# First loads in a fixed order with z's first units cut in halves, and the last output tile added and stored in halves, in a hybrid decoder block on one core

## The chip, the core and the metric

The kernel runs on one core of a Trainium2 chip. The core has five engines with instruction streams of their own: TensorE (PE in the profile; its weight loads are PEld), VectorE (DVE), ScalarE (ACT), GpSimd (POOL) and SyncE (SP), which here only issues transfers. Transfers are issued by SP, by ACT or by POOL and run on 16 DMA engines. The metric is the device time of one execution in microseconds (us); less is better. The profile is one profiled execution, and its span is the time from its first to its last instruction.

## The reference

One layer of a decoder block, 512 tokens, model width 1024, float32 throughout:

```
u = RMSNorm(x)
[q_A,k_A,v_A,z_A,a_A,b_A | q_B,k_B,v_B,f_B | gate_A,gate_B] = u @ W_in
A: causal conv(4)+SiLU on q/k/v, L2-norm of q and k, gated delta rule in chunks, per-head RMSNorm * SiLU(z)
B: RMSNorm of q and k per head, causal softmax attention with a bias cumsum(log sigmoid(f))
m = sigmoid(gate_A) * (y_A @ P_A) + sigmoid(gate_B) * (y_B @ P_B);  h = x + m @ W_out
out = h + relu(RMSNorm(h) @ W_up)^2 @ W_down
```

## The kernel before

Every product is made in three matmuls of rounded parts: each operand is split into a high part (a cast on ACT, type fp32r) and a low part (a subtraction on DVE), and PE adds high times high, low times high and high times low. The weights come in units of 128 x 1024 numbers (512 KB). `seq` lists the units in the order of their use: first `w_ab` (128 x 256, the gates' columns), then five units of `w_z`, then those of `w_gdn` and so on. A unit is loaded into a `raw` tile (`load`, line 209; three buffers of the pool `wraw`), split into `hi` and `lo` (`prefetch_split`, line 258) and used by `unit` and `dense`.

The front of the kernel runs like this. VectorE sets `ones`, ACT copies one column of it (`warm`, for its table load), and PE runs ten warm-up matmuls (line 320). The gain `mix_g` is loaded by POOL. x comes transposed in eight tiles `xt[k]` of 128 x 512 (256 KB each). The loop at line 334 issues them on SP, and between them `prefetch_raw(2 + k)` loads the first units: behind x's tile 0 come `w_ab` and both halves of the first `w_z` unit (`cuts`, line 238), behind tile 1 both halves of the second, then tiles 2 to 7, then the third `w_z` unit and the small inputs. The loop at line 405 makes, per tile, the product with the gain as a high part on ACT and a low part on DVE (`split`, lines 304 and 305), splits the units that are due (lines 265 to 272), squares the tile on ACT (line 410) and adds the square to `sqs` on DVE (line 412). Behind it stands the first product stage (lines 415 to 422): per tile of x two matmuls for `w_ab` and three for each of the two `w_z` units, 64 in all, into three PSUM banks. Then `sumsq` (line 366) multiplies `sqs` with `ones`, and `gates` turns the sum into the inverse norm `rs`, spreads it by matmuls with `ident` (line 378) and copies it to `rb` (line 379). The z products are multiplied by `rb` on DVE (line 1070), which frees their banks for the following z units, and `normalise` (line 425) multiplies x by `rb` on POOL and splits it again as `uhi` and `ulo` for all later products. `blk_id` (line 355) is made of four small copies on ACT; a matmul at line 495 is its first reader.

The end of the kernel is the list `MLP`, whose last two steps are the product P4 of the last quarter of `w_d`. `tokens_product` (line 1339) makes, for two blocks of 128 tokens (t = 0, 1), six matmuls of 512 columns each per step. `add_product` yields tasks that scale the PSUM banks and add them to the accumulators `accs` (`add_task`, line 1356, on DVE); `count` calls `give` (line 1454) once both are added, which stores both tiles of 256 KB from SP.

The order of instructions on each engine is not that of the code: a planner orders them by times that it estimates itself. Three things bind it: data dependencies, buffers, and `keep_in_program_order`, which ties an instruction behind the one traced before it on its engine.

Of the kernel before, what the change touches and what calls it, by code (L numbers as in the profile page):

```python
# [15 lines left out]
P = 128  # L16
# [28 lines left out]
def hybrid_block(tc, a, out):  # L45
# [39 lines left out]
    def const(shape, s, dt=F32):  # L85
        return (cp if s in KEEP else cm).tile(shape, dt, tag=s, name=s)
# [52 lines left out]
    def start(gen):  # L139
        tasks.append(gen)  # L140
        return gen
# [67 lines left out]
    def load(n):  # L209
        nme, i = seq[n]  # L210
        if nme in FACTOR:
            w, c, s_ = i
            q, old = FACTOR[nme]
            if old is None:
                if w == "w_st" and c >= NST:
                    raw = fresh[{"P1": 1, "P2": 2, "P3": 0}[nme]].tile([P, D], F32, tag="raw", name=nm("sraw"))
                elif w in ("w_st", "w_sf"):
                    raw = (swp if nme == "P1" else wraw).tile([P, D], F32, tag="raw", name=nm("sraw"))
                else:
                    raw = fresh[2 if nme == "P2" else s_].tile([P, D], F32, tag="raw", name=nm("draw"))  # L220
# [17 lines left out]
        cuts = [slice(0, 512), slice(512, D)] if 0 < n < 3 else [slice(0, w)]  # L238
        for c in cuts:
            nc.sync.dma_start(raw[:, c], a[nme][i][:, c])  # L240
        raws[n] = raw, cuts
# [68 lines left out]
    ones = const([P, P], "ones")  # L310
    vec.memset(ones, 1.0)
    warm = const([P, 1], "warm")
    act.copy(warm, ones[:, 0:1])
    expo = const([P, 16], "expo")
    vec.memset(expo, -0.5)
# [3 lines left out]
    for _ in range(NWARM):  # L319
        mm(pw[:, 0:P], ones, ones, start=True, stop=True)  # L320

    def small_in(name, shape, eng=None):
        t = const(shape, "c_" + name)
        (eng or nc.sync).dma_start(t, a[name])
        return t

    def small_row(name, n):
# [1 line left out]
        nc.sync.dma_start(t, a[name].partition_broadcast(P))  # L329
        return t  # L330

    mix_g = small_in("norm_mix_g", [P, KT], nc.gpsimd)
    xt = [page(s="x") for _ in range(KT)]
    for k in range(KT):
        nc.sync.dma_start(xt[k], a["xT"][k])
# [16 lines left out]
    pool.tensor_scalar(mid[:P // 2, :], upper[:P // 2, :], 1.0, None, op0=ALU.subtract)  # L352
    blk_id = const([P, 32], "blk_id")
    for b in range(4):
        act.copy(blk_id[b * 32:(b + 1) * 32, :], ident[b * 32:(b + 1) * 32, b * 32:(b + 1) * 32])
    fqs = const([P, 1], "fqs")
    pool.tensor_scalar(fqs, fq_g, float(P) ** -0.5, None, op0=ALU.mult)

# [42 lines left out]
    for pool_, tag, n in early:  # L401
        t = pool_.tile([P, n * T], F32R, tag=tag, name=nm("xs"))
        spots += [t[:, i * T:(i + 1) * T] for i in range(n)]
    sqs = page(s="proj")
    for k in range(KT):
        xs.append(split(xt[k], mix_g[:, k:k + 1], dst=spots[2 * k:2 * k + 2] if k < 3 else None))
        if k < 2:
            prefetch_split(2 + k)
        sq = page(s="sq") if k else sqs
        act.activation(sq, xt[k], AF.Square)  # L410
        if k:
            vec.tensor_tensor(sqs, sqs, sq, op=ALU.add)
    first = [unit("w_ab"), unit("w_z"), unit("w_z")]
    fps = [mmps() for _ in first]
    for k in range(KT):
# [642 lines left out]
    gt = start(gates(fps[0]))  # L1058
    tick()
    tick()  # L1060
    def zgate(h):
        if h < len(fps) - 1:
            ps = fps[1 + h]
        elif h < NZX:
            ps = dense("w_z", xh, xl)
        else:
            ps = dense("w_z", uh, ul)
        z = page(s="proj")
        if h < NZX:
            vec.tensor_tensor(z, ps, rb, op=ALU.mult)  # L1070
            ps = z
        act.activation(z, ps, AF.Silu)
        nc.sync.dma_start(zd[h], z)
        tick()
# [8 lines left out]
    for h in range(NZ1, H):  # L1083
# [3 lines left out]
    ahead = []  # L1087
    stream(EARLY, [fox_chunk((None, v01), (0, v01[0])), fox_chunk((2, v23[0]), (1, v01[1])), fox_chunk((3, v23[1]), (None, v23))],
           uforms, lambda c: start(decays(1, box)) if c == "d" else ahead.append(project(G, len(ahead))), False)
    hold[0] = True  # L1090
    ch1 = gdn_group(1, box, ahead=ahead)
    hold[0] = False
# [246 lines left out]
    def tokens_product(c, p, s_, form, ps, first):  # L1339
# [114 lines left out]
    def give(i, l):  # L1454
        for tb in (2 * i, 2 * i + 1):
            nc.sync.dma_start(out[tb][:, l * T:(l + 1) * T], accs[tb][l])

    MADE = {"P2": (("P1", "a"), ("P1", "b")), "P6": (("P2", "a"), ("P2", "b")), "P4": SUMS}
    evicted = []
    for k, (w, c, p, s_) in enumerate(MLP):  # L1460
# [27 lines left out]
        if w == "w_u":  # L1488
            if p == "P1" and s_ == 0:
                mlp[c] = quarters("act"), {}  # L1490
            qs, forms = mlp[c]
            blocks_product(c, p, s_, [hforms[k] for k in needs], ps, first)
            evicted = [(evict, p, qs[s_], ps[s_])]
            if s_ == NSUB - 1 and p in MADE:
                steps = MADE[p]
                if p == "P4" and c == NC - 1:
                    steps = sorted(steps, key=lambda st: ("P5", "P6", "P3", "P7", "P4").index(st[0]))
                evicted.append((forms_later, qs, forms, steps))
        else:
            tokens_product(c, p, s_, res[p, s_], ps, first)  # L1500
            done = h_done if w == "w_o" else give if c == NC - 1 else lambda i, l: None
            evicted = list(add_product(w, c, p, ps, done)) if s_ == NSUB - 1 else []
        evicted += gone
    for f, *args in evicted:
        f(*args)
# [81 lines left out]
```

## Time and profile before

| | |
|---|---|
| median of 3 runs | 966.58 us (966.54 to 966.62) |
| profiled execution | 968.33 us |
| its span | 966.5 us |
| mean granted TensorE clock | 0.998 |
| PE busy | 956.0 us (99%) |
| DVE, ACT, POOL busy | 756.2, 645.0, 219.7 us |
| transfers over the span | 180.38 MB |

Busy times are sums over an engine's instructions where they do not overlap. A row of the order of time names the start and the length in us, the engine, the line, the operation, the tile it writes and those it reads; in brackets stands how long the engine had been idle and what ended it. A row of the stage table has the stretch, its length, busy time and number of instructions for PE, PEld, DVE, ACT and POOL, the granted clock, the busy share of the DMA engines and GB/s. A row of the waits has the waiting instruction, what it waited for, us in total, times, and the longest. In the tables of transfers the last number is us from issue to landing.

### The profile page before, as it was taken

To read this page: it belongs to the slowest core of one execution; us is meant where nothing else is said; L and a number is where in the kernel's file an instruction comes from. 1 tells how busy PE (TensorE), PEld (TensorE's weight loads), DVE (VectorE), ACT (ScalarE), POOL (GpSimd) and SP (SyncE) were. 2 spreads that over 40 slices of the span, in tenths; PEclk is the share of its full clock that TensorE was granted. 3 is DMA by queue.
4 is the path that set the end of the run, shared out by engine and by line. 5 is a ranking of instruction groups with operands and counts; after the bars stand their busy time and mean duration, and the time that the engine had idled before them with its cause. 6 is when DMAs were issued, how large, how long until landed. Compare 5 with 4: busy or idle time off the path is not lost.

```text
span 966.5 us, 17529 instructions
## 1 busy us (share of the span) xinstructions
PE 956.0 (99%) x6634; PEld 873.6 (90%) x6634; DVE 756.2 (78%) x1281; ACT 645.0 (67%) x1096; POOL 219.7 (23%) x224
## 2 busy tenths in 40 slices
PE   8999999999999999999999999999999999999998
PEld 6788889988888999999999899889989989988986
DVE  6877979967488899956656887979886796697696
ACT  7879855678675577888655554678755855666761
POOL 1503222340343243322230110202122021121110
PEclk9999999999999999999999999999999999999999
DMA  8457678854677877858789687878798798788883
GB/s 284 138 160 240 189 177 203 175 167 138 202 244 190 181 162 164 190 119 189 202 185 328 143 221 208 152 186 169 172 216 179 194 166 204 183 174 197 192 170 111
DMA packets 87291, 180.38 MB, mean 187 GB/s; under 512 B 8152, under 2 KB 41048, under 8 KB 87208
## 3 DMA queue, kind: packets, MB, share of 16 engines
q0 software_dynamic: 17392, 63.12, 38.0%
q1 hardware_dynamic: 69816, 116.15, 37.1%
q8 instruction: 52, 0.85, 0.3%
q14 instruction: 31, 0.25, 0.1%
HBM read 160.11 MB, written 19.14 MB: 185 GB/s over the span
## 4 chain that ended last, share of the span: by engine, by line
PE 71%; DVE 3%; issue 2%; ACT 2%; DMA 1%; POOL 0%; POOLq 0%; DVEq 0%
PE mlp L1228 36%; PE st L1003 14%; PE mm L290 4%; PE mm L291 4%; PE mm L294 4%; PE fo L963 1%; DMA sraw<-w_st 1%; DVE lo L272 1%; PE o L825 1%; PE v L804 1%; PE w L796 1%; PE o L824 1%; PE S L813 1%; PE pT L954 1%; PE T L749 0%
## 5 line engine op out<-in xcount | busy, mean ns | idle before, releaser
L1472 ACT CAST hi<-draw 128x1024 fp32r<-128x1024 f32 x124 | 130.0, 1050 | 116.7 <-PE mlp L1228 103.2
L1479 DVE TENSOR_TENSOR lo<-draw,hi 128x1024 fp32r<-128x1024 f32 x124 | 151.5, 1223 | 47.0 <-ACT hi L1472 44.5
L271 ACT CAST hi<-sraw 128x1024 fp32r<-128x1024 f32 x84 | 88.1, 1049 | 78.4 <-PE st L1003 44.2
L272 DVE TENSOR_TENSOR lo<-sraw,hi 128x1024 fp32r<-128x1024 f32 x84 | 105.2, 1252 | 26.2 <-ACT hi L271 23.7
L1228 PE MATMUL mlp<-hi,shi 128*128 128x512 f32 x280 | 109.4, 391 | 0.7 <-ACT hi L1472 0.6
L1228 PE MATMUL mlp<-hi,slo 128*128 128x512 f32 x280 | 109.1, 390 | 0.0
L1228 PE MATMUL mlp<-lo,shi 128*128 128x512 f32 x280 | 109.0, 389 | 0.0
L1228 PE MATMUL mlp<-slo,hi 128*128 128x256 f32 x448 | 90.3, 283 | 0.0
L1228 PE MATMUL mlp<-shi,lo 128*128 128x256 f32 x448 | 90.3, 283 | 0.0
L1228 PE MATMUL mlp<-shi,hi 128*128 128x256 f32 x448 | 90.3, 283 | 0.0
L291 PE MATMUL mm<-ulo,hi 128*128 128x512 f32 x216 | 84.7, 394 | 1.3 <-DVE ulo L305 1.3
L290 PE MATMUL mm<-uhi,hi 128*128 128x512 f32 x216 | 84.7, 396 | 0.1
L1003 PE MATMUL st<-hi,hi 128*128 128x256 f32 x432 | 73.1, 288 | 0.0
L1003 PE MATMUL st<-hi,lo 128*128 128x256 f32 x432 | 71.6, 284 | 0.0
L1228 PEld LDWEIGHTS mlp<-shi,hi 128*128 128x128 f32 x448 | 70.6, 192 | 0.9
L1003 PE MATMUL st<-lo,hi 128*128 128x256 f32 x432 | 71.3, 285 | 0.0
L1228 PEld LDWEIGHTS mlp<-shi,lo 128*128 128x128 f32 x448 | 69.9, 192 | 0.0
L1228 PEld LDWEIGHTS mlp<-slo,hi 128*128 128x128 f32 x448 | 69.8, 192 | 0.0
L232 POOL DMA_DIRECT2D sraw<-w_st x36 | 32.0, 889 | 161.1 <-DVE lo L272 106.7
L272 DVE TENSOR_TENSOR lo<-raw,hi 128x1024 fp32r<-128x1024 f32 (+1 forms) x42 | 50.9, 1214 | 18.9 <-ACT hi L271 16.9
L1228 PEld LDWEIGHTS mlp<-hi,shi 128*128 128x128 f32 x280 | 52.6, 188 | 11.8 <-ACT hi L1472 0.8
L1228 PEld LDWEIGHTS mlp<-lo,shi 128*128 128x128 f32 x280 | 52.6, 188 | 11.0
(353 smaller groups left out, 2347.4 us busy)
## 6 DMA issues: line engine op xcount, KB each, us to landing
sraw<-w_st POOLq DMA_DIRECT2D x36, 512.0 KB, 6.3
draw<-w_u POOLq DMA_DIRECT2D x32, 512.0 KB, 6.0
draw<-w_d POOLq DMA_DIRECT2D x32, 512.0 KB, 5.9
sraw<-w_st SPq DMA_DIRECT2D x27, 512.0 KB, 5.1
draw<-w_d SPq DMA_DIRECT2D x26, 512.0 KB, 4.4
raw<-w_gdn SPq DMA_DIRECT2D x24, 512.0 KB, 4.1
draw<-w_u SPq DMA_DIRECT2D x24, 512.0 KB, 4.5
hd<-hd SPq DMA_DIRECT2D x34, 256.0 KB, 4.5
```

What stands on the lines that cost most here:

```text
L232: nc.gpsimd.dma_start(raw, a[w][c, q, s_], accum_op=ALU.add)
L271: act.copy(hi[:, c], raw[:, c])
L272: vec.tensor_tensor(lo[:, c], raw[:, c], hi[:, c].bitcast(F32), op=ALU.subtract)
L290: mm(o, w, rhi(k), start=(k == 0), stop=False)
L291: mm(o, w, rlo(k), start=False, stop=False)
L294: mm(o, lo[:, k * cols:(k + 1) * cols], rhi(k), start=False, stop=(k == KT - 1))
L796: mm(pw[:, cs(i)], ks[i], st[:, cs(i)], start=True, stop=True)
L804: mm(pv[:, cs(i)], AT[:, i * NCH + c, :], vs[i], start=True, stop=True)
L1003: mm(o, u, w, start=first and t == 0 and k == 0 and j == 0 and x is hi, stop=x is lo and k == 3, skip_group_check=True)
L1228: return (lambda *args, **kw: tc.keep_in_program_order(f(*args, **kw))) if self.pinned[0] else f
L1472: pact.copy(hi, raws[m][0])
L1479: pvec.tensor_tensor(lo, raws[m][0], hi[:, :].bitcast(F32), op=ALU.subtract)
```

## The change

At the front:

- The gain `mix_g` is issued from ACT instead of POOL, ahead of everything else there.
- The first loads get an order of their own, each tied behind the one before on its queue. On SP: x's tile 0, `w_ab`, the first half of the first `w_z` unit, x's tiles 1 to 3, the second halves of both `w_z` units, x's tiles 4 to 7. From ACT: the gain, then the first half of the second `w_z` unit.
- Whatever else SP issues until the end of the first part of attention is tied behind x's last tile (`issue_after`: order of issue only, no wait for its end).
- Splitting x, splitting the units and the squares are tied to the order of the code on ACT and DVE. The first halves of the `w_z` units are split in quarters of 256 columns, with x's tiles 0 and 1, their second halves with tile 3. The square of tile k stands behind the split of tile k+1.
- `blk_id` is copied on POOL instead of ACT.

At the end, for the very last step of the list: the six matmuls of the second block of tokens become twelve of 256 columns, first all of the left half, then all of the right. Its accumulator is added and stored in these halves, the first block's as a whole.

```diff
+    keep = tc.keep_in_program_order
+    mix_g = const([P, KT], "c_norm_mix_g")
+    keep(nc.scalar.dma_start(mix_g, a["norm_mix_g"]))
+    PIECES = [slice(0, 256), slice(256, 512), slice(512, D)]
...
+    def first_load(n, c, eng=nc.sync):
+        nme, i = seq[n]
+        keep(eng.dma_start(raws[n][0][:, c], a[nme][i][:, c]))
...
+    x_load(0)
+    first_load(2, slice(0, 512), nc.scalar)
+    first_load(0, PIECES[0])
+    first_load(1, slice(0, 512))
+    for k in range(1, 4):
+        x_load(k)
+    for n in (1, 2):
+        first_load(n, PIECES[2])
+    for k in range(4, KT):
+        last = x_load(k)
+    behind_x = ExitStack()
+    behind_x.enter_context(tc.issue_after(last.ins))
     act.copy(warm, ones[:, 0:1])
...
-    for k in range(KT):
-        nc.sync.dma_start(xt[k], a["xT"][k])
-        if k < 2:
-            prefetch_raw(2 + k)
...
-        act.copy(blk_id[b * 32:(b + 1) * 32, :], ident[b * 32:(b + 1) * 32, b * 32:(b + 1) * 32])
+        pool.tensor_copy(blk_id[b * 32:(b + 1) * 32, :], ident[b * 32:(b + 1) * 32, b * 32:(b + 1) * 32])
...
+    def piece(n, c):
+        (hi, lo), raw = units[n], raws[n][0]
+        keep(act.copy(hi[:, c], raw[:, c]))
+        keep(vec.tensor_tensor(lo[:, c], raw[:, c], hi[:, c].bitcast(F32), op=ALU.subtract))
...
     for k in range(KT):
-        xs.append(split(xt[k], mix_g[:, k:k + 1], dst=spots[2 * k:2 * k + 2] if k < 3 else None))
-        if k < 2:
-            prefetch_split(2 + k)
-        sq = page(s="sq") if k else sqs
-        act.activation(sq, xt[k], AF.Square)
+        hi, lo = spots[2 * k:2 * k + 2] if k < 3 else (page(F32R, "hi")[:, :], page(F32R, "lo")[:, :])
+        keep(act.activation(hi, xt[k], AF.Copy, scale=mix_g[:, k:k + 1]))
+        keep(vec.scalar_tensor_tensor(lo, xt[k], mix_g[:, k:k + 1], hi.bitcast(F32), op0=ALU.mult, op1=ALU.subtract))
+        xs.append((hi, lo))
+        if k == 0:
+            keep(act.copy(h3[:, :, 0:32], r3))
+            keep(vec.tensor_tensor(h3[:, :, 32:64], r3, h3[:, :, 0:32].bitcast(F32), op=ALU.subtract))
+        for n in (1, 2) if k in (0, 1, 3) else ():
+            piece(n, PIECES[(0, 1, None, 2)[k]])
         if k:
-            vec.tensor_tensor(sqs, sqs, sq, op=ALU.add)
+            square(k - 1)
+    square(KT - 1)
...
+            if t and apart_halves:
+                for h in halves:
+                    for f in range(2):
+                        k, wc = slice(f * 256 + P, f * 256 + 2 * P), slice(f * T + h.start, f * T + h.stop)
+                        for a, b in ((shi, whi), (slo, whi), (shi, wlo)):
+                            ppe.matmul(ps[t][:, h], a[:, k], b[:, wc], start=False, stop=f == 1 and b is wlo,
+                                       skip_group_check=True)
+                continue
...
+    def add_last(ps):
+        for tb, h in ((2, slice(0, T)), (3, halves[0]), (3, halves[1])):
+            yield add_task, accs[tb][0][:, h], ps[tb - 2][:, h], ALU.add, r2_h[:, 0, tb:tb + 1]
+            yield send, tb, 0, h
```

More of the change, by code (lines that the diff above doesn't have):

```diff
@@ L237, in load @@
         raw = wraw.tile([P, D], F32, tag="raw", name=nm("raw"))
-        cuts = [slice(0, 512), slice(512, D)] if 0 < n < 3 else [slice(0, w)]
+        cuts = [slice(0, w)]
         for c in cuts:
@@ L312, in hybrid_block, with x_load @@
     warm = const([P, 1], "warm")
+    keep = tc.keep_in_program_order
+    mix_g = const([P, KT], "c_norm_mix_g")
+    keep(nc.scalar.dma_start(mix_g, a["norm_mix_g"]))
+    xt = [page(s="x") for _ in range(KT)]
+    for n in range(3):
+        raws[n] = wraw.tile([P, D], F32, tag="raw", name=nm("raw")), None
+    PIECES = [slice(0, 256), slice(256, 512), slice(512, D)]
+    def first_load(n, c, eng=nc.sync):
+        nme, i = seq[n]
+        keep(eng.dma_start(raws[n][0][:, c], a[nme][i][:, c]))
+    def x_load(k):
+        return keep(nc.sync.dma_start(xt[k], a["xT"][k]))
+    x_load(0)
[10 more added lines that the diff above has]
+    behind_x.enter_context(tc.issue_after(last.ins))
     act.copy(warm, ones[:, 0:1])
@@ L320, in hybrid_block, with small_in @@
         mm(pw[:, 0:P], ones, ones, start=True, stop=True)
-    def small_in(name, shape, eng=None):
+    def small_in(name, shape):
         t = const(shape, "c_" + name)
-        (eng or nc.sync).dma_start(t, a[name])
+        nc.sync.dma_start(t, a[name])
         return t
@@ L330, in small_row @@
         return t
-    mix_g = small_in("norm_mix_g", [P, KT], nc.gpsimd)
-    xt = [page(s="x") for _ in range(KT)]
-    for k in range(KT):
-        nc.sync.dma_start(xt[k], a["xT"][k])
-        if k < 2:
-            prefetch_raw(2 + k)
     prefetch_raw(4)
@@ L404, in hybrid_block, with square @@
     sqs = page(s="proj")
-    for k in range(KT):
-        xs.append(split(xt[k], mix_g[:, k:k + 1], dst=spots[2 * k:2 * k + 2] if k < 3 else None))
-        if k < 2:
-            prefetch_split(2 + k)
-        sq = page(s="sq") if k else sqs
-        act.activation(sq, xt[k], AF.Square)
+    for n in range(3):
+        hi = whl.tile([P, D], F32R, tag="hi", name=nm("hi"))
+        units.append((hi, whl.tile([P, D], F32R, tag="lo", name=nm("lo")) if n else None))
+    h3, r3 = v3(units[0][0][:, 0:512], KT), v3(raws[0][0][:, 0:256], KT)
+    def piece(n, c):
+        (hi, lo), raw = units[n], raws[n][0]
+        keep(act.copy(hi[:, c], raw[:, c]))
+        keep(vec.tensor_tensor(lo[:, c], raw[:, c], hi[:, c].bitcast(F32), op=ALU.subtract))
+    def square(k):
+        sq = page(s="sq") if k else sqs
+        keep(act.activation(sq, xt[k], AF.Square))
+        if k:
+            keep(vec.tensor_tensor(sqs, sqs, sq, op=ALU.add))
+    for k in range(KT):
+        hi, lo = spots[2 * k:2 * k + 2] if k < 3 else (page(F32R, "hi")[:, :], page(F32R, "lo")[:, :])
[7 more added lines that the diff above has]
+            piece(n, PIECES[(0, 1, None, 2)[k]])
         if k:
-            vec.tensor_tensor(sqs, sqs, sq, op=ALU.add)
+            square(k - 1)
+    square(KT - 1)
     first = [unit("w_ab"), unit("w_z"), unit("w_z")]
@@ L1089, in hybrid_block @@
            uforms, lambda c: start(decays(1, box)) if c == "d" else ahead.append(project(G, len(ahead))), False)
+    behind_x.close()
     hold[0] = True
@@ L1337, in banks, with tokens_product @@
         return [t for t, _ in banks_of[w, c, b]], first, [(banks_back, (w, c, b))] if gone else []
-    def tokens_product(c, p, s_, form, ps, first):
+    halves = slice(0, 256), slice(256, T)
+    def tokens_product(c, p, s_, form, ps, first, apart_halves=False):
         whi, wlo = units[pos[0] - 1]
@@ L1456, in give, with send @@
             nc.sync.dma_start(out[tb][:, l * T:(l + 1) * T], accs[tb][l])
+    def send(tb, l, h):
+        nc.sync.dma_start(out[tb][:, l * T + h.start:l * T + h.stop], accs[tb][l][:, h])
+    def add_last(ps):
+        for tb, h in ((2, slice(0, T)), (3, halves[0]), (3, halves[1])):
+            yield add_task, accs[tb][0][:, h], ps[tb - 2][:, h], ALU.add, r2_h[:, 0, tb:tb + 1]
+            yield send, tb, 0, h
     MADE = {"P2": (("P1", "a"), ("P1", "b")), "P6": (("P2", "a"), ("P2", "b")), "P4": SUMS}
@@ L1499, in hybrid_block @@
         else:
-            tokens_product(c, p, s_, res[p, s_], ps, first)
+            ends = k == len(MLP) - 1
+            tokens_product(c, p, s_, res[p, s_], ps, first, ends)
             done = h_done if w == "w_o" else give if c == NC - 1 else lambda i, l: None
-            evicted = list(add_product(w, c, p, ps, done)) if s_ == NSUB - 1 else []
+            evicted = list(add_last(ps) if ends else add_product(w, c, p, ps, done)) if s_ == NSUB - 1 else []
         evicted += gone
```

## The prediction

> **What bounds the kernel now.** I read the busy times first, then one table by stage, then the waits of TensorE (PE), then the order of time at both ends.
>
> ```profile
> span 966.5 us, 17529 instructions
> PE 956.0 (99%) x6634; PEld 873.6 (90%) x6634; DVE 756.2 (78%) x1281; ACT 645.0 (67%) x1096; POOL 219.7 (23%) x224
> 0.00:10.00 10.00, 7.41 (x28) 5.60 (x29) 3.92 (x8) 7.12 (x15) 2.75 (x11) 1.00 0.78 250
> 50.00:650.00 600.00, 598.08 (x4431) 552.24 (x4431) 469.33 (x921) 409.22 (x771) 149.65 (x141) 1.00 0.73 188
> 650.00:960.00 310.00, 310.00 (x1996) 283.94 (x1996) 248.12 (x297) 197.22 (x266) 54.22 (x62) 1.00 0.82 182
> 960.00:966.50 6.50, 2.40 (x11) 1.67 (x9) 1.50 (x2) 0.00 (x0) 0.00 (x0) 0.90 0.21 81
> PE mm L291 <- DVE ulo L305: 1.3, 1, 1.3
> ```
>
> In the stage rows the first number behind the comma is PE's busy time. Of 10.5 us without a matmul, 2.6 lie in the first ten and 4.1 in the last 6.5; in the 910 us from 50 to 960 PE lacks 1.9. So the change can earn something only at the two ends it touches, and what it earns at the front reaches the end only if the middle keeps its order.
>
> The front, PE in order of time (start, length), with ACT, DVE and the SP queue:
>
> ```profile
> 1.05 4.63 PE L320 MATMUL warm<-ones 128*128 128x128 f32 x20 [1.05 <-DVE expo L315]
> 5.83 0.52 PE L417 MATMUL mm<-xs,hi 128*64 128x512 f32 x1
> 8.76 0.45 PE L417 MATMUL mm<-xs,hi 128*64 128x512 f32 x1 [1.05 <-ACT xs L304]
> 9.79 0.50 PE L420 MATMUL mm<-xs,hi 128*128 128x512 f32 x1 [0.35 <-ACT hi L271]
> 10.13 0.40 PE L421 MATMUL mm<-xs,hi 128*128 128x512 f32 x1
> 23.07 1.00 PE L366 MATMUL ss<-ones,proj 128*128 128x64 f32 x8
> 5.06 0.72 ACT L304 ACTIVATE xs<-x,c_norm_mix_g 128x512 fp32r<-128x512 f32 x1 [0.62 <-DMA c_norm_mix_g<-norm_mix_g]
> 7.99 0.72 ACT L304 ACTIVATE xs<-x,c_norm_mix_g 128x512 fp32r<-128x512 f32 x1 [0.63 <-DMA x<-xT]
> 19.34 0.69 DVE L412 TENSOR_TENSOR proj<-proj,sq 128x512 f32<-128x512 f32 x1
> 2.59 0.43 SPq L335 DMA_DIRECT2D x<-xT  x1
> x<-xT SPq DMA_DIRECT2D x1, 256.0 KB, 5.4
> 6.00:8.00 2.00, 1.72 (x5) 0.64 (x5) 1.77 (x3) 0.92 (x3) 0.00 (x0) 1.00 1.07 367
> ```
>
> The first product stage has 64 matmuls, eight for each of x's eight tiles. The ninth starts at 10.13, the first thing behind the last (L366) at 23.07: 56 in 12.94 us, 0.231 each, with no gap. The first eight take 4.30 us where eight steps are 1.85, so the stage loses 2.45 us, all before 10.13. The loss has a name: ACT sits until x's second tile lands at 7.99 (issued at 2.59, 5.4 us on its way, behind four other transfers), and PE starts on it at 8.76. Ahead of it had gone both halves of the first z unit, of which the second half is needed only from x's fifth tile on. From 6 to 8 us the transfer engines are full at 367 GB/s (last two numbers of the stage row), so the order of bytes matters.
>
> **The change, part by part.** *Order of the first loads.* Before the second x tile SP now issues x's first, w_ab and z's first half-unit; the second z unit's half goes out from ACT. Ahead of it lie the same 256+128+256+256 KB as before, only that the last 256 are now ones that PE can use. If bytes decide, the tile lands again at 7.99. If its place in SP's queue decides, it lands one issue earlier: 0.43 us, so 7.56. I take 7.56, since the engines were not full all the time before (next row: 143 GB/s, share 0.76), and keep 7.99 as one end.
>
> ```profile
> 3.00:4.50 1.50, 1.50 (x9) 1.50 (x9) 0.04 (x1) 1.27 (x4) 0.85 (x2) 1.00 0.76 143
> ```
>
> PE starts the tile 8.76-7.99 = 0.77 us after landing: 8.33. By then all eight matmuls of the first tile can be done, not five as before: they cannot begin before the warm-up ends at 5.68, and from there eight steps with two slow ones (0.5 each, as the first row at 5.83 has it) end at about 8.1. So 56 steps are left: 8.33+12.94 = 21.27, and 23.07-21.27 = 1.8 us are won. With the tile at 7.99 it is 21.70, a gain of 1.37; with everything in time 8.1+12.94 = 21.04, a gain of 2.03, which is the ceiling that the warm-up sets.
>
> The Trainium skill, page "DMA: Bandwidth & Descriptors", section "Issuing engines are not separate DMA queues", says that transfers from several engines share the same 16 DMA engines and that a second issuer saves only issue time. By that rule the ACT queue moves no byte sooner once the engines are full, and the gain would be nearer 1.37; the share of 1.07 at 6 to 8 us agrees with it, the 0.76 at 3 to 4.5 leaves room.
>
> ```profile
> 0.73 1.28 ACT L313 ACT_TABLE_LOAD   x1 [0.73 <-PEq L1579]
> 2.46 0.90 ACT L355 COPY blk_id<-ident 32x32 f32<-32x32 f32 x4 [0.25 <-POOL ident masks.py:199]
> 4.04 0.39 ACT L265 CAST hi<-raw 128x256 fp32r<-128x256 f32 x1
> 10.17 0.72 ACT L304 ACTIVATE xs<-x,c_norm_mix_g 128x512 fp32r<-128x512 f32 x1
> 11.32 0.71 ACT L304 ACTIVATE hi<-x,c_norm_mix_g 128x512 fp32r<-128x512 f32 x1
> 1.29 0.73 POOL L324 DMA_DIRECT2D c_norm_mix_g<-norm_mix_g  x1 [0.36 <-issue]
> c_norm_mix_g<-norm_mix_g POOLq DMA_DIRECT2D x1, 4.0 KB, 3.7
> c_norm_mlp_g<-norm_mlp_g SPq DMA_DIRECT2D x1, 4.0 KB, 1.6
> 15.88 0.56 POOL L357 TENSOR_SCALAR fqs<-c_fox_q_norm_g 128x1 f32<-128x1 f32 x1 [11.93 <-DMA c_fox_q_norm_g<-fox_q_norm_g]
> ```
>
> *The fixed order of ACT and DVE.* Per x tile ACT does one product with the gain (xs, L304) and one square, 1.15 from one L304 to the next in these rows, plus the casts of z in quarters. Between x's second and third tile lie that pair and two casts of 256 columns (0.39 each, as w_ab's): from 7.56 to 9.49, then the third xs until 10.21, its DVE part (about 0.7, as DVE's row of this width at 19.34) until 10.9. PE wants that tile at 8.33+1.85 = 10.18 and its low part one step later, unless the five matmuls that need only the high part go first, which are 1.15 us. So between 0 and 0.5 is lost; I take 0.2. Then ACT (1.15 per tile) outruns PE (1.85). Squares come one tile later than now; the sum of squares ended at 20.03 (19.34+0.69) and was wanted at 23.07. Now it is wanted at about 21.4, and the last square ends no later with the same work on ACT: 1.4 us of cover, none of it lost unless ACT stalls so long.
>
> *Two DMA issues on ACT* (0.4 each by SP's row) push the table load to about 1.6 to 2.9. It lies in front of the first xs; the four copies of blk_id leave ACT (0.90) for POOL, which sits 11.93 us in front of L357. Nothing on the path. *The gain vector* goes from POOL at 1.29 (landed 3.7 later, 5.0) to ACT at 0.7; a transfer of its size from a hardware queue took 1.6, so 2.3 to 4.4. It released the first xs; that now waits for x's first tile, but PE is in its warm-up until 5.68, so this is worth at most 0.15 and is in the ceiling already. *Other loads behind x*: in the code of before too SP reaches them only behind x's last tile, so this moves nothing; if one of them came sooner or later, the next stage's casts cover it, which wait for buffers that PE frees.
>
> *What comes next* must move forward with the stage. The chain behind it:
>
> ```profile
> 29.59 1.05 PE L378 MATMUL rb<-ident,rs 128*128 128x128 f32 x8
> 31.30 1.29 DVE L1070 TENSOR_TENSOR proj<-mm,rb 128x512 f32<-128x512 f32 x2 [0.23 <-ACT rb L379]
> 32.04 0.51 PE L290 MATMUL mm<-xs,hi 128*128 128x512 f32 x1 [0.40 <-DVE proj L1070]
> ```
>
> Each link hangs on the PE work in front, none on a clock of its own, so all of it moves by the same amount. But apart from the pinned part the order of instructions is set by a planner with its own times, which is run anew. No row of before can price that. Its bounds: PE lacks 3.8 us between 10 and 960 (10.5 less 2.6 and 4.1), so little more than one long wait (1.3, L291) can go; and as much can come. I take 0 with 1.0 either way.
>
> *The last tile in halves.*
>
> ```profile
> 214.76 2.87 PE st L1003 x24
> 962.01 0.39 PE L1228 MATMUL mlp<-lo,shi 128*128 128x512 f32 x1
> 962.44 0.75 DVE L1356 SCALAR_TENSOR_TENSOR acc<-mlp,r_h,acc 128x512 f32<-128x512 f32 x1 [0.61 <-PE mlp L1228]
> L651 DVE SCALAR_TENSOR_TENSOR AT<-kk,ssk,eb x32: 334/341/350, 82.2 to 336.9; 128x128 f32<-128x128 f32 x32
> 964.00:965.00 1.00, 0.00 (x0) 0.00 (x0) 0.00 (x0) 0.00 (x0) 0.00 (x0) 1.00 0.69 262
> 54.81 0.33 PE L526 MATMUL cum<-gf,tri 128*128 128x64 f32 x2
> 54.98 0.39 PE L527 MATMUL cum<-gf,ones 128*128 128x64 f32 x2
> 55.40 0.22 DVE L528 COPY gates<-cum 128x64 f32<-128x64 f32 x1 [1.34 <-PE cum L527]
> ```
>
> Six matmuls of 512 columns (step 0.227) become twelve of 256; 24 of that width take 2.87, so twelve take 1.43 instead of 1.36: 0.07 later. An add of 512 takes 0.75 and one of 128 takes 0.34, so one of 256 takes about 0.48. The last store's data moves in 0.69 us (share of the row times its 1 us); a half takes 0.35. If the first half's add runs while the second half is multiplied, the end comes 0.27 (add) plus 0.35 (store) less 0.07 earlier: 0.55. But the rows at 54.8 speak against it: L528 reads columns that L526 had written by 55.14, and yet started at 55.40, 0.03 behind the end of L527, which writes other columns of the same PSUM bank. If the halves wait like that, both adds follow the last matmul: 0.07+0.48+0.43 instead of 0.75, 0.23 later, against 0.35 on the store. I take 0.1 earlier, between 0.55 earlier and 0.25 later (the store not shorter at all).
>
> The Trainium skill, page "PSUM — Partial Sum Buffer", section "PSUM bank collisions raise a hardware error", says that two engines on one bank collide also in disjoint columns, so that a bank must be guarded whole. By that rule the halves' adds cannot overlap the matmuls, which gives the 0.1 and not the 0.55; the 55.40 above agrees.
>
> **Sum.** Front 1.8 less 0.2, end 0.1, middle 0: 1.7 us off the profiled execution, 968.33 us (span 966.5), so 966.6. The median of the runs shown is 966.58, 1.75 below that execution; the same step gives 964.9.
>
> **The rivals.** *A. The halves overlap after all and the front reaches its ceiling*: 2.03+0.55 = 2.6, so 964.0. For it: the matmuls of the halves are written as separate groups. Against it: L528. *B. The order brings little*: z's second half-unit, sent from ACT beside x's first tile, takes its share of the engines, and ACT, in a fixed order, casts both z pieces before it touches x's second tile. If that lands at 8.8 instead of 7.56, PE starts it at 9.57 and the gain is 0.56, less the 0.2: 0.4, so 966.2. For it: the full engines at 6 to 8 us. Against it: the same bytes were ahead of it before. *C. Slower*: the planner's new order puts more of the gates' small DVE work ahead of `ulo` (L305), for which PE waits once, 1.3 us. Each further such wait costs 1.3; two eat the gain of 1.7 (967.5 at 0.9 above the median), and from three on the kernel is slower by over 0.2% (968.8). For it: this part is not pinned. Against it: the inputs of that stage all move together, and so do the planner's times for it.
>
> **How the numbers follow.** 0.2% is 1.93 us, about what a measurement of this kernel can tell from no change: 964.65 and 968.51 are the bounds. The forecast with its bounds (front 1.2 to 2.0, end -0.25 to 0.35, middle within 0.5) holds 0.55 and gives 964.0 to 965.7, a good quarter of it below 964.65. A has 0.15, B 0.12, C 0.08, of which half is over the upper bound; a middle that gains by its new order (to 963.5) has 0.10. Faster: 0.16+0.13+0.10 = 0.39; slower 0.04; the rest, 0.57, within. Range: 963.5 to 966.7, from the gaining middle to a little past B.
>
> **What the profile of the changed kernel would show.** PE's step from x's first to second tile at about 8.3 without a gap above 0.3 behind it; L366 at 21.2 to 21.7; the `rb` matmuls as much earlier, 1.4 to 1.9; TensorE's idle time between 50 and 960 again near 2 us; the two adds of the last tile both behind the last matmul; three stores at the end, the last of 128 KB. The prediction is wrong if x's second tile lands past 8.5, if PE's first matmul comes later than 5.9, if the 0.231 step of the first stage breaks (ACT too late), or if new idle time over 1 us stands between 30 and 60 or around a load in the middle.

## The result and the profile after

The changed kernel takes 966.25 us (median of 22 runs, 964.44 to 968.84) against 967.72 us for the kernel before (22 runs beside them, 966.37 to 968.6): ratio 0.9986, 95% interval 0.9979 to 0.9992, or 1.5 us less. That is inside 0.2%, with a reliable sign. The forecast was 1.7 us less. Its absolute time, 964.9, was reckoned from a median of 966.58; the kernel before came out at 967.72 here, so only the difference can be compared.

Both kernels' runs spread over 2 us and more for a reason of their own: in some executions the granted clock halves for some 3.4 us at one or two places in the middle (below). A run lists its mean granted clock; where I compare "runs at full clock", I mean those with 0.999 or more. Among those the changed kernel's median is 965.09 (12 runs). The clocks of the 22 runs before are not on record, so I take the nine of them below 967 us: median 966.56 (966.37 to 966.76), again 1.47 more. The clock is not the whole of the scatter: two of the changed kernel's twelve, 966.94 and 967.32, ran at 1.00, and why they are 2 us longer is open.

The profiled execution of the changed kernel took 968.5 us, no less than the 968.33 of before. The page and the table by stage (columns as in the prediction) say where that comes from:

```profile
span 966.7 us, 17548 instructions
PE 956.7 (99%) x6640; PEld 875.0 (91%) x6640; DVE 756.4 (78%) x1284; ACT 645.1 (67%) x1094; POOL 221.9 (23%) x227
```

```profile
0.00:10.00 10.00, 8.27 (x36) 6.93 (x37) 3.88 (x10) 6.16 (x12) 2.85 (x14) 1.00 0.79 270
...
40.00:50.00 10.00, 8.52 (x29) 6.29 (x28) 9.45 (x22) 9.56 (x15) 0.03 (x1) 0.83 0.29 79
50.00:650.00 600.00, 598.05 (x4432) 552.18 (x4432) 467.62 (x919) 407.88 (x768) 151.19 (x141) 1.00 0.74 188
650.00:960.00 310.00, 310.00 (x1995) 283.91 (x1994) 247.78 (x297) 197.26 (x266) 54.39 (x62) 1.00 0.83 182
410.00:430.00 20.00, 19.44 (x281) 18.41 (x279) 12.01 (x26) 16.23 (x34) 5.51 (x5) 0.91 0.52 129
```

In the first ten us PE is now busy for 8.27 instead of 7.41, and from 50 to 960 nothing has changed (598.05 and 310.00 against 598.08 and 310.00). But from 40 to 50 us the clock column reads 0.83: this execution ran part of the stage at half speed (1.00 in the profile before).

The front in order of time (rows picked out), and behind it two rows of the table of transfers:

```profile
2.12 1.38 SPq L327 DMA_DIRECT2D x<-xT  x3
5.22 0.41 ACT L449 CAST hi<-raw 128x256 fp32r<-128x256 f32 x1 [0.74 <-DMA raw<-w_ab]
6.14 0.45 PE L460 MATMUL mm<-xs,hi 128*64 128x512 f32 x1 [0.68 <-DVE hi L450]
7.16 0.73 ACT L445 ACTIVATE xs<-x,c_norm_mix_g 128x512 fp32r<-128x512 f32 x1
8.29 0.39 PE L460 MATMUL mm<-xs,hi 128*64 128x512 f32 x1
10.15 0.40 PE L460 MATMUL mm<-xs,hi 128*64 128x512 f32 x1
21.23 1.00 PE L388 MATMUL ss<-ones,proj 128*128 128x64 f32 x8
27.74 1.05 PE L400 MATMUL rb<-ident,rs 128*128 128x128 f32 x8
30.19 0.50 PE L291 MATMUL mm<-xs,hi 128*128 128x512 f32 x1 [0.40 <-DVE proj L1114]
```

```profile
raw<-w_ab SPq DMA_DIRECT2D x1, 128.0 KB, 4.0
c_norm_mix_g<-norm_mix_g ACTq DMA_DIRECT2D x1, 4.0 KB, 3.0
```

PE makes its ninth matmul, the first of x's second tile, at 8.29, and enters the third tile at 10.15, eight steps later with no gap (a row without brackets had no idle time ahead). Before, the ninth came at 10.13; the second tile had been entered at 8.76, but with three products of the first still to make. The sum of squares starts at 21.23 instead of 23.07, 1.84 sooner, and the chain behind it keeps that: `rb` 27.74 for 29.59, the next z products 30.19 for 32.04. What PE waits for in front has changed too: the first matmul comes at 6.14 instead of 5.83, behind `w_ab`, which needed 4.0 us to land.

The longest wait of PE in the middle, the end in order of time, and the last stores in the table of transfers, of the changed kernel and (second row) of the one before:

```profile
PE mm L292 <- DVE ulo L306: 1.3, 1, 1.3
```

```profile
960.91 0.75 DVE L1411 SCALAR_TENSOR_TENSOR acc<-mlp,r_h,acc 128x512 f32<-128x512 f32 x1 [2.67 <-PE mlp L1273]
961.68 1.97 SPq L1514 DMA_DIRECT2D out<-acc  x3
962.02 0.28 PE L1273 MATMUL mlp<-lo,shi 128*128 128x256 f32 x1
962.34 0.88 DVE L1411 SCALAR_TENSOR_TENSOR acc<-mlp,r_h,acc 128x256 f32<-128x256 f32 x2 [0.68 <-PE mlp L1273]
```

```profile
out<-acc SPq DMA_DIRECT2D x2, 128.0 KB, 1.8
```

```profile
out<-acc SPq DMA_DIRECT2D x2, 256.0 KB, 2.0
```

The long wait for `ulo` stands as it stood. At the end both halves' adds follow the last matmul (962.30) as one stretch of 0.88 us, where the whole add took 0.75. From the end of the last matmul to the end of the span are 4.40 us (966.70 − 962.30) against 4.10 before (966.50 − 962.40): the end became 0.3 worse in these two profiles. Over all profiles below it takes 4.03 to 4.22 us with the tile as a whole and 4.30 to 4.40 with halves in one bank and three stores, so 0.1 to 0.3 worse.

### The profile page after: what moved, and what is told of

It reads as the page before. It is cut to its first block, busy times and chain, and to the rows that moved or that the text cites. A ratio compares the mean times of both kernels' runs of the same rounds, so it can differ in the third digit from the quotient of the medians.

```text
span 966.7 us, 17548 instructions
## 1 busy us (share of the span) xinstructions
PE 956.7 (99%) x6640; PEld 875.0 (91%) x6640; DVE 756.4 (78%) x1284; ACT 645.1 (67%) x1094; POOL 221.9 (23%) x227
## 4 chain that ended last, share of the span: by engine, by line
PE 71%; DVE 3%; issue 2%; ACT 2%; DMA 1%; POOL 0%; DVEq 0%; POOLq 0%
PE mlp L1273 36%; PE st L1046 14%; PE mm L291 4%; PE mm L292 4%; PE mm L295 4%; PE fo L1006 1%; DMA sraw<-w_st 1%; DVE lo L273 1%; PE o L868 1%; PE v L847 1%; PE o L867 1%; PE w L839 1%; PE S L856 1%; PE pT L997 1%; PE T L792 0%
## 5 line engine op out<-in xcount | busy, mean ns | idle before, releaser
L1273 PE MATMUL mlp<-hi,shi 128*128 128x512 f32 (+1 forms) x282 | 109.8, 389 | 0.7 <-ACT hi L1535 0.6
L1273 PE MATMUL mlp<-hi,slo 128*128 128x512 f32 (+1 forms) x282 | 109.5, 388 | 0.0
L1273 PE MATMUL mlp<-lo,shi 128*128 128x512 f32 (+1 forms) x282 | 109.3, 388 | 0.0
L1046 PE MATMUL st<-hi,lo 128*128 128x256 f32 x432 | 71.5, 284 | 0.0
L1273 PEld LDWEIGHTS mlp<-hi,slo 128*128 128x128 f32 x282 | 53.0, 188 | 10.2
```

Source lines behind the costliest of these rows:

```text
L1046: mm(o, u, w, start=first and t == 0 and k == 0 and j == 0 and x is hi, stop=x is lo and k == 3, skip_group_check=True)
L1273: return (lambda *args, **kw: tc.keep_in_program_order(f(*args, **kw))) if self.pinned[0] else f
```

## The experiments

One table first, since most verdicts rest on it. "Front" is the start of the sum of squares, "middle" the time from there to the end of the last matmul, "tail" from there to the end of the span, each of the profiled execution; "clock" is the granted clock of 410 to 430 us (and of 40 to 50 where it is not 1.00). Runs at full clock: median (number).

| kernel | front | middle | clock | tail | median, all runs | at full clock |
|---|---|---|---|---|---|---|
| before | 23.07 | 939.33 | 0.91 | 4.10 | 967.72 | 966.56 |
| changed | 21.23 | 941.07 | 0.91, 0.83 | 4.40 | 966.25 | 965.09 (12) |
| e1, front alone | 21.07 | 939.21 | 0.91 | 4.22 | 964.85 | 964.53 (9) |
| e2, end alone | 22.83 | 939.41 | 0.91 | 4.36 | 967.52 | 967.20 (7) |
| e3, two banks | 21.39 | 937.93 | 1.00 | 3.88 | 965.42 | 964.77 (7) |
| e4, z's second unit from SP | 21.48 | 937.72 | 1.00 | 4.30 | 966.93 | 965.71 (6) |
| e5, old order, tied | 23.01 | 937.79 | 1.00 | 4.20 | 967.25 | 965.95 (4) |
| e6, new order, not tied | 20.97 | 937.76 | 1.00 | 4.17 | 966.27 | 965.01 (5) |
| e7, fill | 20.77 | 939.84 | 1.00 | 4.19 | 966.95 | 966.95 (11) |
| e8, w_ab from ACT | 22.49 | 939.28 | 0.91 | 4.03 | 966.40 | 965.45 (6) |
| e9, two banks, one store | 20.76 | 938.07 | 1.00 | 3.97 | 965.17 | 964.72 (8) |
| e10, one store | 20.95 | 939.36 | 0.91 | 4.19 | 965.21 | 964.76 (8) |

The kernel before, run beside e1 to e4, e5 to e8, and e9 and e10, had medians of 967.14, 967.69 and 966.79 over all runs, and 966.49, 966.75 and 966.48 at full clock: all runs move by nearly 1 us between the three with the share of clock drops, those at full clock by 0.27. I lean on the last column and on the profile. There is one profile of each kernel, and the same front does not always end at the same time: five executions of the changed front ended it between 20.76 and 21.39, two of the front before at 22.83 (e2) and 23.07.

**e1: the front alone.**

```diff
-            tokens_product(c, p, s_, res[p, s_], ps, first, ends)
+            tokens_product(c, p, s_, res[p, s_], ps, first)
...
-            evicted = list(add_last(ps) if ends else add_product(w, c, p, ps, done)) if s_ == NSUB - 1 else []
+            evicted = list(add_product(w, c, p, ps, done)) if s_ == NSUB - 1 else []
```

> The changed kernel with its end undone: the last tile is multiplied, added and stored as a whole. Theory 1 (the whole gain is made at the front): the sum of squares starts on TensorE at 21.2 us as in the changed kernel (23.07 before), and the time is within 0.4 us of the changed kernel's, some 1.5 us below the kernel before. Rival (the halves at the end carry 0.5 us or more of it): the front still ends at 21.2, but the time is 0.5 us or more above the changed kernel's.

Ratio 0.9973 (0.9963 to 0.9984); 1.96 less at full clock. PE goes from the warm-up straight into the first tile and from that into the second (order of time):

```profile
5.62 0.69 PE L460 MATMUL mm<-xs,hi 128*64 128x512 f32 x1
8.13 0.39 PE L460 MATMUL mm<-xs,hi 128*64 128x512 f32 x1
...
21.07 1.00 PE L388 MATMUL ss<-ones,proj 128*128 128x64 f32 x8
...
959.89 0.39 PE L1273 MATMUL mlp<-lo,shi 128*128 128x512 f32 x1
960.32 0.75 DVE L1411 SCALAR_TENSOR_TENSOR acc<-mlp,r_h,acc 128x512 f32<-128x512 f32 x1 [0.61 <-PE mlp L1273]
```

The front alone brings all of the gain, and more than the whole change does: at full clock it is 0.56 below the changed kernel, past the 0.4 expected, and on the side away from the rival.

**e2: the end alone.** The kernel before with the change's twelve matmuls, `add_last` and `send`, and its own front.

> The kernel before with only the last tile in halves. Theory 1: the two adds of the halves both start behind the last matmul, since they share its PSUM bank, and from the end of the last matmul to the end of the span it takes 4.1 us plus or minus 0.3, as before; time within 0.3 us of the kernel before. Rival (the halves overlap or the shorter store pays): 0.5 us below the kernel before.

Ratio 1.000 (0.999 to 1.001). No gain: 0.7 more at full clock, 0.1 more in the profiled execution (968.4 for 968.33, both with one clock drop), so the cost lies between nothing and 0.7. The tail of 4.36 is inside the expected 4.1 ± 0.3, the time at full clock is not inside the expected 0.3. The end has the same form as in the changed kernel:

```profile
961.96 0.28 PE L1228 MATMUL mlp<-lo,shi 128*128 128x256 f32 x1
962.28 0.88 DVE L1366 SCALAR_TENSOR_TENSOR acc<-mlp,r_h,acc 128x256 f32<-128x256 f32 x2 [0.68 <-PE mlp L1228]
```

The run shows something about the old front too. Its rows of ACT and PE there:

```profile
7.28 0.72 ACT L304 ACTIVATE xs<-x,c_norm_mix_g 128x512 fp32r<-128x512 f32 x1
9.08 0.50 PE L420 MATMUL mm<-xs,hi 128*128 128x512 f32 x1 [0.34 <-ACT hi L271]
10.78 0.44 PE L417 MATMUL mm<-xs,hi 128*64 128x512 f32 x1 [0.27 <-ACT xs L304]
```

x's second tile was there by 7.28, 0.7 sooner than in the other profile of this front, yet the sum of squares started only 0.24 sooner (22.83). PE now waited for the cast of the second z unit and again for x's third tile. So the old stall did not hang on x's second tile alone.

**e3: the right half in a PSUM bank of its own**, in both last steps of the list:

```diff
+            if (w, c, p) == ("w_d", NC - 1, "P4"):
+                banks_of[w, c, b].append(bank_new("mlp"))
...
+                    o = ps[1][:, h] if h is halves[0] else ps[2][:, 0:256]
...
-                            ppe.matmul(ps[t][:, h], a[:, k], b[:, wc], start=False, stop=f == 1 and b is wlo,
+                            ppe.matmul(o, a[:, k], b[:, wc], start=s_ == 0 and f == 0 and a is shi and b is whi,
```

> The changed kernel, with the right half of the last tile accumulated in a PSUM bank of its own, in both of the last two steps. Theory 1 (a reader waits for all writes to its bank): the left half's add now starts while the right half is multiplied, about 0.5 us ahead of the last matmul's end, the right half's add is the only one behind it, and the end comes 0.3 to 0.6 us earlier than in the changed kernel (tail 3.8 to 4.0 us instead of 4.4). Rival (the adds are late for another reason, such as the planner's order): both adds still follow the last matmul and nothing moves.

```profile
7.56 0.72 ACT L445 ACTIVATE xs<-x,c_norm_mix_g 128x512 fp32r<-128x512 f32 x1 [1.34 <-DMA x<-xT]
8.33 0.45 PE L460 MATMUL mm<-xs,hi 128*64 128x512 f32 x1 [0.53 <-ACT xs L445]
...
958.64 0.48 DVE L1414 SCALAR_TENSOR_TENSOR acc<-mlp,r_h,acc 128x256 f32<-128x256 f32 x1
959.04 0.28 PE L1273 MATMUL mlp<-lo,shi 128*128 128x256 f32 x1
959.36 0.48 DVE L1414 SCALAR_TENSOR_TENSOR acc<-mlp,r_h,acc 128x256 f32<-128x256 f32 x1 [0.23 <-PE mlp L1273]
```

Ratio 0.9982 (0.9969 to 0.9994). Now the left half's add (958.64 to 959.12) runs while the right half is multiplied (until 959.32), and only the right half's 0.48 follows. The tail falls from 4.40 to 3.88: the common bank is what had lined the adds up. The first two rows are dealt with below.

**e4: z's second unit from SP.** Its first half behind the first unit's on SP, nothing but the gain from ACT.

```diff
-    first_load(2, slice(0, 512), nc.scalar)
     first_load(0, PIECES[0])
     first_load(1, slice(0, 512))
+    first_load(2, slice(0, 512))
```

> The changed kernel, with the first half of the second z unit issued from SP behind the first unit's, instead of from ACT. Theory 1 (bytes decide, and the half from ACT only shared the engines with w_ab): w_ab lands at about 4 us instead of 5.2, TensorE's first product starts at 5.5 to 5.8 instead of 6.14, x's second tile is issued 0.45 later and lands at 7.1 to 7.6, and the front ends between 20.9 and 21.6. Rival (the second queue is what brought the tile forward): x's second tile lands at 7.9 or later, a gap of 0.5 us or more opens in front of it on TensorE, and the front ends at 21.7 or later.

Ratio 0.999 (0.9979 to 1.0001). The front was within the numbers of theory 1 (21.48) and `w_ab` was there by 4.37 us, and x's second tile landed at 7.63, at the edge of the expected 7.1 to 7.6 and short of the rival's 7.9. But the first product came later than the expected 5.5 to 5.8:

```profile
6.50 0.50 PE L463 MATMUL mm<-xs,hi 128*128 128x512 f32 x1 [0.92 <-ACT hi L434]
```

The planner, run anew, put a z product ahead of `w_ab`'s, and z's piece was cast only at 6.04. Against the changed kernel the front is 0.25 later in these two profiles and the time 0.6 higher at full clock (965.71 and 965.09), but how much of that is the second issuer and how much the planner's new order, this run does not tell. What it does show is that most of the earlier front in its profile needs no second queue.

**e5 and e6: the ties and the order apart.** e5 issues the bytes in the order of before, with the ties, the gain from ACT and `blk_id` on POOL; e6 has the new order of bytes with no ties on ACT and DVE. Both end with a whole last tile.

```diff
 e5:
+    x_load(0)
+    first_load(0, PIECES[0])
+    first_load(1, slice(0, 512))
+    first_load(1, PIECES[2])
+    x_load(1)
+    first_load(2, slice(0, 512))
+    first_load(2, PIECES[2])
+    for k in range(2, KT):
 e6:
-        keep(act.copy(hi[:, c], raw[:, c]))
+        act.copy(hi[:, c], raw[:, c])
...
-        keep(act.activation(hi, xt[k], AF.Copy, scale=mix_g[:, k:k + 1]))
+        act.activation(hi, xt[k], AF.Copy, scale=mix_g[:, k:k + 1])
```

> The changed front with a whole last tile, but its first loads in the order of the kernel before, all from SP (x's tile 0, w_ab, both halves of the first z unit, tile 1, both halves of the second z unit, tiles 2 to 7); ACT and DVE stay tied to the new order of work. Theory 1 (the order of the bytes makes the gain; the ties alone do not): ACT now waits for the second z unit's first half, which landed at 8.7 us in the kernel before, ahead of x's second tile, so TensorE starts that tile at 9.5 to 9.9 and the front ends at 22.4 to 22.9: within 0.6 us of the kernel before. Rival (the ties are what helped): the front ends at 21.7 or earlier.

> The changed front with a whole last tile and the new order of loads, but ACT's and DVE's work on the first tiles left to the planner. Theory 1 (the order of the bytes makes the gain): the front ends at 21.0 to 21.7. Rival (without the ties the planner lets work whose data land late go first on ACT): the front ends at 22.0 or later, with idle time of 0.5 us or more on TensorE between 5.5 and 10 us.

e5: ratio 0.9995 (0.9986 to 1.0004), front 23.01, just past the expected 22.4 to 22.9. e6: 0.9987 (0.9977 to 0.9996), front 20.97. The starts of the sum of squares, e5 first, then e6:

```profile
23.01 1.00 PE L387 MATMUL ss<-ones,proj 128*128 128x64 f32 x8
```

```profile
20.97 1.00 PE L388 MATMUL ss<-ones,proj 128*128 128x64 f32 x8
```

In the profiles the order of the loads is the gain, and the ties are not needed for it and cost nothing that shows. The runs at full clock are less clear-cut: against the kernel before beside them (966.75) e6 is 1.74 lower, e5 0.80 (four runs, of which the profiled one, 966.78, is the longest). So by these medians the order is worth some 0.9 us of it, and the rest may be what e5 keeps of the change (ties, gain from ACT, `blk_id` on POOL), the planner's new order, or landings that vary; that stays open. e5 shows what the ties do with the old bytes: ACT sits for the second z unit and PE with it.

```profile
8.80 0.40 ACT L433 CAST hi<-raw 128x256 fp32r<-128x256 f32 x1 [3.12 <-DMA raw<-w_z]
9.25 0.50 PE L462 MATMUL mm<-xs,hi 128*128 128x512 f32 x1 [2.09 <-ACT hi L433]
```

**e7: fill PE where the clock drops.** The front alone, plus nine matmuls of `ones` with `ones` whose results nobody reads: five in the first dense product behind the inverse norm, where PE waits for `ulo`, and four ahead of the chunks' 32 x 32 inversions near 416 us.

```diff
+            if fill and k == 3:
+                for _ in range(5):
+                    keep(mm(pf[:, 0:P], ones, ones, start=True, stop=True))
...
+        if filled.count("T") == 2:
+            for x in (*pqs, *pqs):
+                mm(x[:, 0:P], ones, ones, start=True, stop=True)
```

> The changed front with a whole last tile, plus nine matmuls of ones whose results nobody reads: five of them in the place where TensorE waits 1.3 us for ulo in the first w_gdn product, four in front of the small 32x32 matmuls of the second group's inversion. Theory (the scatter of the times comes from the granted clock, which falls to half for some 3 us behind stretches with little TensorE work): the mean clock is 0.999 or more in all runs but one or two, and the runs lie within 1 us; the lowest times stay within 0.8 us of those without the fill. Rival (the clock falls for another reason): a third of the runs or more still have a clock of 0.998 or less and are 1.5 us longer.

Ratio 0.9995 (0.9987 to 1.0004). The scatter is gone: 11 of 11 runs at full clock, all within 1.2 us (1 was expected), where in the changed kernel and the nine other variants 54 of 126 runs were below 0.999. The hoped-for time is not: its lowest run is 966.46, 2.2 above e1's lowest (964.24) where I had expected 0.8 at most. The middle is 939.84, 2 us above the 937.7 to 938.1 of undropped profiles. The added matmuls themselves can account for that: the first five hold PE from 70.51 to 71.62, 0.22 each, so nine would take 2.0 (an estimate). And the first five did not go where I meant them: the tile `fill` is written at 70.5 to 71.5 us, and the 1.3 us wait for `ulo` is still there. So which of the two groups keeps the clock up is not told by this run.

**e8: w_ab from ACT too**, ahead of z's half, whole last tile:

```diff
+    first_load(0, PIECES[0], nc.scalar)
     first_load(2, slice(0, 512), nc.scalar)
-    first_load(0, PIECES[0])
```

> The changed front with a whole last tile; w_ab is issued from ACT behind the gain, and the second z unit's first half behind w_ab, so that SP has only x's tile 0 and the first z half ahead of x's tile 1. Theory 1 (once the bytes are in order, TensorE's own 64 steps behind the warm-up bound the front): the front ends at 20.9 to 21.4, no more than 0.2 us better than with w_ab from SP (21.07 to 21.39). Rival (the landing of w_ab and of x's tile 1 still bounds it): x's tile 1 lands 0.4 us sooner and the front ends below 20.9.

Ratio 0.9987 (0.9978 to 0.9995), front 22.49: neither theory's number. `w_ab` is cast at 4.69 and PE starts at 5.45, but then:

```profile
8.05 0.40 ACT L434 CAST hi<-raw 128x256 fp32r<-128x256 f32 x1 [2.65 <-DMA raw<-w_z]
8.51 0.50 PE L463 MATMUL mm<-xs,hi 128*128 128x512 f32 x1 [1.69 <-ACT hi L434]
```

z's half, now behind `w_ab` on ACT's queue, is the late one, and x's second tile stands behind its cast in ACT's tied order. The stall moved from one piece to the next.

**e9 and e10: is the half store worth anything?** The halves added apart, but the block stored once as a whole, with two banks (e9) and with one (e10):

```diff
-            yield send, tb, 0, h
+            if h is not halves[0]:
+                yield send, tb, 0, slice(0, T)
```

> The changed kernel with the right half of the second block in a PSUM bank of its own, both halves added apart, but the whole 256 KB stored once, behind the second add. Theory 1 (what ends the kernel behind the last add is a fixed time, about 3.3 to 3.4 us, whatever the store's size): from the end of the last matmul to the end of the span 3.8 to 3.95 us, as with two stores (3.88), and a median 0 to 0.3 below that of the kernel with two banks and two stores. Theory 2 (a store of half the size does save, but a second store issued just ahead of it gives that back): 3.9 to 4.2 us, the store taking about 0.2 longer than the one of 128 KB. Both: the first matmuls and the start of the sum of squares as in the changed kernel, 20.9 to 21.5.

> The changed kernel with both halves in one PSUM bank, added apart, but stored once as a whole. Theory 1 (fixed time behind the last add): both adds again behind the last matmul, and from its end to the end of the span 0.88 to 0.95 + 3.3 to 3.4 = 4.2 to 4.35 us, no later than with two stores (4.40). Theory 2 (the half store saves up to 0.35): 4.5 to 4.75.

e9: ratio 0.9982 (0.9971 to 0.9992); e10: 0.998 (0.9969 to 0.999). Their ends, e9's two rows first:

```profile
958.55 0.28 PE L1273 MATMUL mlp<-lo,shi 128*128 128x256 f32 x1
958.87 0.48 DVE L1414 SCALAR_TENSOR_TENSOR acc<-mlp,r_h,acc 128x256 f32<-128x256 f32 x1 [0.23 <-PE mlp L1273]
```

```profile
960.03 0.28 PE L1273 MATMUL mlp<-lo,shi 128*128 128x256 f32 x1
960.35 0.88 DVE L1411 SCALAR_TENSOR_TENSOR acc<-mlp,r_h,acc 128x256 f32<-128x256 f32 x2 [0.68 <-PE mlp L1273]
```

From the end of the last add to the end of the span: 962.8 − 959.35 = 3.45 in e9 (3.36 with two stores, e3), 964.5 − 961.23 = 3.27 in e10 (3.48 in the changed kernel). Over all twelve profiles it is 3.24 to 3.48, with 256 KB last as with 128 KB. A half store saves nothing that shows. Nor is it shown that the extra store costs anything: with one bank the tail is 4.30 to 4.40 with three stores (three profiles) and 4.19 with two, with two banks it is 3.88 and 3.97. e10's tail of 4.19 is at the lower edge of theory 1's numbers (4.2 to 4.35), and e9's 3.97 just past them (3.8 to 3.95) and inside theory 2's 3.9 to 4.2. The medians at full clock (964.72 and 964.77 for e9 and e3) do not tell the two theories apart there. e9's front, 20.76, is a little below the expected 20.9.

The best of these beat the changed kernel by 0.3 to 0.6 us at full clock (e1 964.53, e9 964.72, e10 964.76, e3 964.77); among themselves they are not to be told apart.

## Why the prediction was right, and where two terms were off

The total came out (−1.5 for −1.7) partly because two errors cancel. With the clock drops taken out, the profiles close the account: front −1.84, tail +0.30, middle 937.9 against 937.8 (941.07 less 1.5 and 1.7 for its two drops; 939.33 less 1.5 for the one of before; their prices are in the last section), together −1.5, as in the runs. That it closes to a tenth is partly chance: with another of the five executions of the changed front it would be −1.3 to −2.0.

**The front's mechanism held.** In the profiles of e5 and e6 the order of the loads decides; how much of the time the runs ascribe to it is said there. I took 1.8 less 0.2; five executions of the same front (the changed kernel, e1, e3, e9, e10) gave 21.23, 21.07, 21.39, 20.95 and 20.76, which is 1.7 to 2.3 sooner than 23.07, 1.84 in the changed kernel's own profile.
- *Landing of x's second tile.* Forecast 7.56 with PE on it at 8.33. In e3 that is what happened (the rows at 7.56 and 8.33), but to the hundredth only by luck: in four other executions of the same front ACT had the tile between 6.30 and 7.16, so its place in SP's queue is not all that sets its landing. In the changed kernel's own profile the tile was there by 7.16 and PE still came to it at 8.29, for another reason: it had begun its first tile only at 6.14, behind `w_ab`. That both fell near 8.3 is a coincidence. When the same front gets both in time (e1) it falls at 8.13, the forecast's ceiling of about 8.1.
- *The first matmul past 5.9* stood among the signs of a failure. It came at 6.14 and nothing failed: this wait took the place of part of the old stall, which I had not named as what is late next. `w_ab` took 4.0 us to land here and 2.7 before; in the four other executions of this front it took 3.1 to 3.8, and in e1 it was cast at 4.37. Why its landing varies is not settled; e8 shows that issuing it on ACT, just ahead of z's half, makes z's half late instead.
- *The name of the loss* was too narrow. I put it all down to x's second tile; e2's rows show that the second z unit's half and x's third tile held PE up as well. The new order moves the z half up too, which is why the gain came all the same.
- *The 0.2 for ACT* at x's third tile was not lost: the row at 10.15 has no idle time ahead of it.
- *The ceiling of 2.03* was too low: e9 reached 2.31 (20.76). I had priced two slow steps of 0.5 into the first tile; in e9 its eight steps took 1.92 (5.91 to 7.83).

**The middle** was taken as 0 ± 1 from the planner's new order. That is right to 0.4 us across profiles of the same clock (937.72 to 938.07, and 939.21 to 939.41; e7's added matmuls left out), and no new wait appeared, so rival C had no footing; nor did B, whose late x tile did not come. What I had not priced is the granted clock, which moves a single run by more than the change does.

**The end** was forecast 0.1 better and is 0.3 worse in the profile (0.1 to 0.3 over all profiles). The step on the PSUM bank was right: both adds follow the last matmul, 0.88 for 0.75 (0.13 more, where 0.16 of the forecast's 0.23 was for them and 0.07 for the twelve matmuls), and e3 shows that the bank is the cause, so rival A's overlap needs a second bank. The Trainium skill, page "PSUM — Partial Sum Buffer", section "PSUM bank collisions raise a hardware error", has the rule that predicted it (guard by the bank, not by the columns), and the trace agrees: 0.88 behind the last matmul with one bank, 0.48 with two. The term that failed is the store. I took its transfer time (0.69) as proportional and all on the path: 0.35 less. It landed in 1.8 us instead of 2.0, and the end of the span did not follow even that: from the last add's end 3.48 us passed with the half and 3.31 with the whole. SP issued three stores in place of two; whether the extra one costs anything is not shown (e10 against e9, above). I had kept "the store not shorter at all" as an end of the range; it was the answer. What fills the last 1.3 to 1.6 us, from the landing (issue about 963.3 plus 1.8 in the changed kernel, 963.2 plus 2.0 before) to the end, the profile does not show.

## What to carry to other kernels

When a front is held up by loads, list what the first product needs, piece by piece, and issue in that order; a piece needed some tiles later must not stand ahead of one needed now, and a fixed order of work on the engines did not replace that in e5's profile and was not needed for it in e6. After each move ask which piece is now the last to land, since another takes its place (e4, e8). Splitting the last tile shortened the tail here only with its halves in different PSUM banks (3.88 and 3.97 us against 4.03 to 4.22 for the whole tile), too little to show in the medians beside e1's, and a smaller last store is worth what the end of the span shows, not what its bytes suggest.

## What was not expected of the hardware

The granted clock drops in the middle of a busy kernel, in some executions and not in others of the same kernel. Stage rows of the changed kernel (four), of before, of e1 and of e9:

```profile
46.00:48.00 2.00, 2.00 (x7) 1.51 (x6) 1.85 (x7) 2.00 (x3) 0.00 (x0) 0.51 0.81 290
48.00:50.00 2.00, 2.00 (x7) 1.62 (x6) 2.00 (x4) 2.00 (x5) 0.00 (x0) 0.63 0.03 9
418.00:420.00 2.00, 2.00 (x48) 1.94 (x46) 1.84 (x2) 2.00 (x8) 0.00 (x0) 0.53 0.03 8
420.00:422.00 2.00, 2.00 (x13) 2.00 (x12) 0.58 (x3) 1.11 (x3) 0.00 (x0) 0.62 0.78 193
```

```profile
420.00:422.00 2.00, 2.00 (x12) 2.00 (x11) 0.68 (x3) 1.20 (x3) 0.00 (x0) 0.50 0.70 186
```

```profile
410.00:430.00 20.00, 19.44 (x264) 18.50 (x258) 12.07 (x26) 16.21 (x34) 6.16 (x5) 0.91 0.41 110
```

```profile
410.00:430.00 20.00, 19.46 (x272) 18.52 (x265) 12.89 (x29) 17.73 (x37) 6.16 (x5) 1.00 0.50 118
```

The drop near 420 costs about 1.5 us, as the middles in the table show: 937.7 to 938.1 without it, 939.2 to 939.4 with it. That at 46 leaves out 2 x 0.49 + 2 x 0.37 = 1.7 us of full speed by its two rows, and the middle with both is 941.07. The one at 418 leaves out 2 x 0.47 + 2 x 0.38 = 1.7 us as well; at half speed that is some 3.4 us each time. They come right behind thin stretches of PE's work: the one at 46 behind the 1.33 us wait for `ulo`, that near 420 behind a wait of 0.55 us and some 2 us of 32 x 32 matmuls.

```profile
44.71 0.50 PE L292 MATMUL mm<-ulo,hi 128*128 128x512 f32 x1 [1.33 <-DVE ulo L306]
```

The Trainium skill, page "TensorE: Matmul & The Clock Gate", section "Part 1: The HAM clock gate", says that the clock falls to half after an idle window of about 3.4 us that runs freely, so that one kernel behaves differently from run to run. The half rate and the change from run to run agree with the 0.50 and the table above; the idle time does not, since no wait of PE near the two places is longer than 1.33 us. That the thin stretches are the cause is supported by e7, whose added work left no run below 0.999; it is not shown stretch by stretch. A thin stretch alone is not enough: the other eleven profiles have a wait of 1.1 to 1.3 us for `ulo` in the forties too, and a clock of 1.00 there.
